# Half-array matmuls of a two-block layer: the later half issued first, the other half queued directly behind it

## The chip, the cores and the metric

The kernel runs on one core of a Trainium2 chip. The metric is the device time of one execution in microseconds (us). The core's engines are PE (TensorE, the matmul array; PEld is its weight load), DVE (VectorE), ACT (ScalarE), POOL (GpSimd) and SP (SyncE). Each engine works through its own queue of instructions in order, and semaphores order one engine against another.

## The reference

256 tokens of width 1024, float32, go through two blocks. What matters here:

```python
# first block: x += 0.5*ffn1(x); mixer = attention + mLSTM; x += 0.5*ffn2(x); norm
scores = einsum('bnqhgd,bnkhd->bhgnqk', qb, kb) * 64**-0.5   # window 128, 16 heads, 4 kv heads, width 64
probs  = softmax(concat([scores, sink]))[..., :-1]
out    = einsum('bhgnqk,bnkhd->bnqhgd', probs, vb)
sc     = einsum('bhtd,bhsd->bhts', q_, k_) * w_intra         # mLSTM, 8 heads, q/k width 64, values 128
...
# second block: mixer = gated linear attention + latent attention; cross attention; ffn with conv
sc = einsum('bhqd,bhkd->bhqk', qi, kf) * 96**-0.5            # latent attention, 8 heads
p  = softmax(where(causal, sc, -inf))
o  = einsum('bhqk,bhkd->bqhd', p, vf)                        # values of width 64
```

## The kernel before

The kernel is one long chain of matmuls. Every dense weight is read from memory as float32 (SP's queue, tiles `wr`), split into a high part `wh` on ACT (line 376) and a low part `wl` on DVE (line 377), and multiplied in two or three matmuls (lines 396 to 407). The tiles `wr`, `wh` and `wl` rotate over six buffers each. Between these weight matmuls stand the small matmuls of the attentions and of the mLSTM.

Four places use only half of the 128 by 128 array, because a head has width 64. They come in pairs, one half for each of two heads:

- Line 719, the first attention's scores. The contraction has 64 rows, rows 0 to 63 for h = 0 and 64 to 127 for h = 1. The two heads write two PSUM banks, `ps[0]` and `ps[1]`.
- Line 759, the first attention's values. The contraction has all 128 rows, and the output has 64 columns of the array, partitions 0 to 63 of `po` for h = 0 and 64 to 127 for h = 1. The moving operand `pTs[2 * kb + h]` is 512 wide. It is written by ACT (line 753), which copies four transposes (line 751) out of PSUM; the copy for h = 1 comes after that for h = 0.
- Line 868, the mLSTM's products of queries and keys, again 64 rows for each head.
- Line 1245, the latent attention's values, 64 columns for each head, with three matmuls of 128 columns per head; the moving operand `pTs[i]` is copied by ACT (line 1240) after the transposes of line 1238.

Lines 1298 and 1322 are half- or quarter-array matmuls of the gated linear attention that the change leaves as they are.

These matmuls are float32 and each stands as two records in the trace: the 12 value matmuls of line 759 are 24 records, the 32 score matmuls of line 719 are 64. The weight matmuls are one record each.

What sets the order of the work: the program is written in the order of the code, and the framework (`TileContext(..., schedule_with_timeline_sim=True)`) then puts each engine's instructions into a fixed order by simulating when each one could run. It may put instructions of other stages between two that stand next to each other in the code. `tc.issue_after(ins)` adds an edge for this placing: what is written inside the block comes later than `ins` in the queue of the same engine. It adds no semaphore. PSUM is two tiles `mm` of two banks each for the weight matmuls and four banks `at` for the small ones.

The first attention runs in four units (p, b), two kv heads each; `scores` of the next unit is written ahead of `values` of the current one. Its matmuls stand between the weight matmuls of the mLSTM's projections. The latent attention does the same with four pairs of heads.

Of the kernel before, what the change touches and what calls it, by code (L numbers as in the profile page):

```python
# [19 lines left out]
P = 128  # L20
D = 1024
KD = D // P
T = 256
# [164 lines left out]
class Builder:  # L188
# [135 lines left out]
                                fill=0.0, base=0, channel_multiplier=-1)  # L324

    @contextmanager
    def queued(self, *engines):

        done = self.nc.cur_bb.bb.instructions
        with ExitStack() as st:  # L330
            for e in engines:
                st.enter_context(self.tc.issue_after(next(i for i in reversed(done) if i.engine == e.engine)))
            yield
# [178 lines left out]
    def mean(self, acc, tag):  # L512

        ps = self.pa()
        self.sums(ps, 0, acc)
        v = self.tmp([P, TB], tag, bufs=1)
        self.nc.vector.tensor_scalar(v, ps[:, :TB], 1.0 / D, None, ALU.mult)
        return v

    def sums(self, ps, i, acc):  # L520

# [138 lines left out]
    def mix(self):  # L660
        nc = self.nc
# [3 lines left out]
        with self.phase("mix") as mp:  # L665
# [20 lines left out]
            aq = [[], []]  # L686
# [4 lines left out]
            ak = biased(product("ak", "ak"), 8)  # L691
            av = mt([P, TB, 256], "av")
            zg = mt([P, TB, 16], "zg")
            bb = self.row("b_av", 0, 272, "bb")
            ps = self.lin_n("av", 272, xs)
# [12 lines left out]
            def scores(p, b):  # L708
                nk = P * (b + 1)
                Ss = mt([P, 2, 4, T], ("ya", "nu")[b])  # L710
                Ss = [Ss[:, h] for h in range(2)]
                ms = [self.tmp([P, 4], "m4", bufs=4) for h in range(2)]
                per = 512 // nk
                for g in range(4 // per):
                    ps = [self.pa() for h in range(2)]
                    for i in range(per):
                        for h in range(2):
                            hs = slice(64 * h, 64 * h + 64)
                            nc.tensor.matmul(ps[h][:, i * nk:i * nk + nk], aq[p][g * per + i][hs, b * P:b * P + P],  # L719
                                             ak[p][hs, 0:nk], start=True, stop=True)  # L720
                    for h in range(2):
                        for i in range(per):
                            j = g * per + i
                            nc.vector.tensor_tensor_reduce(
                                Ss[h][:, j, :nk], ps[h][:, i * nk:i * nk + nk], wm[:, P * (1 - b):2 * P], 0.125, -3.0e38,
                                ALU.add, ALU.max, ms[h][:, j:j + 1])
                for h in range(2):
                    S, m, kv = Ss[h], ms[h], 2 * p + h
                    nm = self.tmp([P, 4], "nm4")
                    nc.vector.scalar_tensor_tensor(nm, m, -1.0, nsink[:, 4 * kv:4 * kv + 4], ALU.mult, ALU.min)  # L730
                    es = self.tmp([P, 4], "es4")
                    nc.vector.tensor_tensor(es, nm, sink[:, 4 * kv:4 * kv + 4], ALU.add)
                    nc.scalar.activation(es, es, AF.Exp)
                    l = self.tmp([P, 4], "l4")
                    for j in range(4):
                        nc.scalar.activation(S[:, j, :nk], S[:, j, :nk], AF.Exp, bias=nm[:, j:j + 1],
                                             accum_out=l[:, j:j + 1])
                    nc.vector.tensor_tensor(l, l, es, ALU.add)
                    r = self.tmp([P, 4], "r4")
                    nc.vector.reciprocal(r, l)  # L740
                    for j in range(4):
                        nc.vector.tensor_scalar(S[:, j, :nk], S[:, j, :nk], r[:, j:j + 1], None, ALU.mult)
                return Ss

            def values(p, b, Ss):
                pTs = []
                for kb in range(b + 1):
                    for h in range(2):
                        pt = self.pa()
                        for j in range(4):  # L750
                            nc.tensor.transpose(pt[:, j * P:j * P + P], Ss[h][:, j, kb * P:kb * P + P], self.ident)  # L751
                        pT = self.tmp([P, 512], "pT", bufs=4)
                        nc.scalar.activation(pT, pt, AF.Copy)
                        pTs.append(pT)
                po = self.pa()
                for kb in range(b + 1):
                    for h in range(2):
                        kv = 2 * p + h
                        nc.tensor.matmul(po[64 * h:64 * h + 64, :], av[:, kb, kv * 64:kv * 64 + 64], pTs[2 * kb + h],  # L759
                                         start=kb == 0, stop=kb == b)  # L760
                self.split(ao[:, :, 4 * p:4 * p + 4, b * P:b * P + P], po.rearrange("p (j t) -> p j t", j=4))

            units = [(p, b) for p in range(2) for b in range(TB)]
# [13 lines left out]
            ps = self.pa()  # L777
# [7 lines left out]
            ps = self.pa()  # L785
# [12 lines left out]
            ps = self.pa()  # L798
# [53 lines left out]
            def weights(m):  # L852

                qt, kt_ = qk[m], qk[4 + m]
                Ws = []
                for h in (2 * m, 2 * m + 1):
                    pw = self.pa()
                    nc.tensor.matmul(pw[:, :3 * P], self.nident[:, h:h + 1].to_broadcast([40, P]), MH, start=True, stop=False)
                    nc.tensor.matmul(pw[:, :3 * P], self.identb, self.kmask.rearrange("p a k -> p (a k)"), start=False, stop=True)
                    W = self.tmp([P, 3 * P], "W", bufs=4)  # L860
                    nc.scalar.activation(W[:, 0:T], pw[:, 0:T], AF.Exp, bias=ga[:, 0, h:h + 1])
                    nc.scalar.activation(W[:, T:3 * P], pw[:, T:3 * P], AF.Exp, bias=ga[:, 1, h:h + 1])
                    Ws.append(W)
                pq = [self.pa() for r in range(2)]
                for a, b, c in ((0, 0, 0), (T, P, P)):
                    for r in range(2):
                        hs = slice(64 * r, 64 * r + 64)
                        nc.tensor.matmul(pq[r][:, a:a + T - b], kt_[hs, b:b + P], qt[hs, c:T], start=True, stop=True)
                for r in range(2):
                    nc.vector.tensor_tensor(Ws[r], pq[r][:, :3 * P], Ws[r], ALU.mult)  # L870
                return Ws
# [195 lines left out]
    def mix2_heads(self, mp, ot, xs, ms):  # L1067
# [165 lines left out]
        def values(hp, Ss):  # L1233
# [7 lines left out]
                pTs.append(pT)  # L1241
            po = self.pa()
            for q0, kb, first, last in ((0, 0, True, True), (P, 0, True, False), (P, 1, False, True)):
                for i in range(2):
                    nc.tensor.matmul(po[64 * i:64 * i + 64, q0:q0 + P], vv[:, kb, 2 * hp + i, :],
                                     pTs[i][:, kb * P + q0:kb * P + q0 + P], start=first, stop=last)
            ms[4 + hp] = ot([P, 2, T], f"mla{hp}", dt=F32R)
            self.split(ms[4 + hp], po[:, :T])

# [64 lines left out]
        st = [None]  # L1314
# [283 lines left out]
```

## Time and profile before

| | |
|---|---|
| median of 3 runs | 1010.16 us (1008.42 to 1011.41) |
| profiled execution | 1012.14 us, of which the trace's span is 1010.4 us |
| PE busy | 992.1 us, 98% of the span |
| DVE / ACT busy | 735.5 us (73%) / 595.2 us (59%) |
| granted TensorE clock, mean | 0.996 |

The trace's times are microseconds from the start of the span. Busy time of PE is the union of its records. A record begins when its matmul starts and lasts until its result is out, so records overlap, and how long a stretch of matmuls takes is read from the start of one row to the start of the next.

### The profile page before, as it was taken

Reading aid. Unit: us, or ns where it says so; the run is one execution under the profiler, and the core shown is the slowest. Engines: PE = TensorE matmul, PEld = TensorE weight load, DVE = VectorE, ACT = ScalarE, POOL = GpSimd, SP = SyncE. Lnnn points to the kernel's source line nnn. Section 1 sums busy time; section 2 is a strip of 40 time slices with the busy share of each in tenths; the row PEclk is TensorE's granted clock in tenths of the full one; section 3 lists DMA queues with packets and bytes.
Section 4 is the critical chain, followed back from the end, with each engine's and each line's share of the span. In section 5 each row is a group of like instructions: output and inputs, shape, how many; then the busy total and the mean of one; then the engine's idle time right before and its main releaser. Section 6 shows DMA issues by size and latency. Waiting matters only on the chain.

```text
span 1010.4 us, 15824 instructions
## 1 busy us (share of the span) xinstructions
PE 992.1 (98%) x5884; PEld 857.2 (85%) x5884; DVE 735.5 (73%) x1289; ACT 595.2 (59%) x1038; POOL 58.3 (6%) x195
## 2 busy tenths in 40 slices
PE   8999999999999999999999999999899999999998
PEld 6888888988677788888888888998688888888887
DVE  6787766668986577776777756768868676998662
ACT  7665544568854556545655644659746465766531
POOL 2100000010000010001000100012001201000000
PEclk9999999999999999999999999999999999999999
DMA  8755555555345335545565655556206235555550
GB/s 307 247 194 187 175 180 178 198 165 181 122 154 188 104 130 204 187 168 174 180 206 189 219 172 185 170 192 211 82 19 211 105 129 204 187 188 178 178 166 21
DMA packets 51405, 172.80 MB, mean 171 GB/s; under 512 B 6256, under 2 KB 7552, under 8 KB 51328
## 3 DMA queue, kind: packets, MB, share of 16 engines
q1 hardware_dynamic: 49536, 169.89, 49.7%
q10 hardware_dynamic: 1728, 1.88, 0.7%
q8 instruction: 46, 0.75, 0.3%
q14 instruction: 31, 0.25, 0.1%
q0 software_dynamic: 64, 0.02, 0.0%
HBM read 170.72 MB, written 1.05 MB: 170 GB/s over the span
## 4 chain that ended last, share of the span: by engine, by line
PE 95%; DVE 2%; ACT 1%; DMA 1%; issue 0%; DVEq 0%; SPq 0%; ACTq 0%
PE mm L400 42%; PE mm L401 21%; PE mm L405 3%; PE mm L406 3%; PE mm L407 3%; PE mm L397 3%; PE mm L396 3%; PE mm L398 3%; PE at L400 1%; PE at L759 1%; PE at L719 1%; DVE wl L377 1%; DMA wr<-in_wts 1%; PE at L401 1%; ACT wh L376 1%; PE at L751 1%
## 5 line engine op out<-in xcount | busy, mean ns | idle before, releaser
L377 DVE TENSOR_TENSOR wl<-wr,wh 128x1024 fp32r<-128x1024 f32 (+5 forms) x376 | 389.6, 1047 | 200.5 <-ACT wh L376 199.1
L376 ACT ACTIVATE wh<-wr 128x1024 fp32r<-128x1024 f32 (+5 forms) x376 | 339.0, 918 | 320.6 <-PE mm L400 159.1
L400 PE MATMUL mm<-xs,wh 128*128 128x512 f32 x1264 | 446.9, 397 | 0.0
L401 PE MATMUL mm<-xs,wl 128*128 128x256 f32 x1264 | 355.2, 281 | 0.8 <-DVE wl L377 0.8
L400 PEld LDWEIGHTS mm<-xs,wh 128*128 128x128 f32 x1264 | 237.6, 188 | 56.8 <-issue 0.7
L401 PEld LDWEIGHTS mm<-xs,wl 128*128 128x128 f32 x1264 | 239.0, 189 | 1.6 <-DVE wl L377 1.1
L400 PE MATMUL mm<-ahl,wh 128*128 128x512 f32 x396 | 140.1, 399 | 0.0
L401 PE MATMUL mm<-ahl,wl 128*128 128x256 f32 x396 | 111.2, 281 | 0.0
L400 PEld LDWEIGHTS mm<-ahl,wh 128*128 128x128 f32 x396 | 74.4, 188 | 18.6
L401 PEld LDWEIGHTS mm<-ahl,wl 128*128 128x128 f32 x396 | 74.8, 189 | 0.0
L406 PE MATMUL mm<-wl,xs 128*128 128x512 f32 (+2 forms) x160 | 61.0, 381 | 0.0
L405 PE MATMUL mm<-wh,xs 128*128 128x512 f32 (+2 forms) x160 | 61.0, 381 | 0.0
L407 PE MATMUL mm<-wh,xs 128*128 128x512 f32 (+2 forms) x160 | 60.7, 379 | 0.0
L400 PE MATMUL mm<-b,wh 128*128 128x512 f32 x128 | 45.4, 395 | 0.0
L397 PE MATMUL mm<-ahl,wh 128*128 128x256 f32 x132 | 37.4, 283 | 0.0
L396 PE MATMUL mm<-ahl,wh 128*128 128x256 f32 x132 | 37.4, 283 | 0.0
L398 PE MATMUL mm<-ahl,wl 128*128 128x256 f32 x132 | 37.3, 283 | 0.0
L401 PE MATMUL mm<-b,wl 128*128 128x256 f32 x128 | 36.5, 285 | 0.0
L406 PEld LDWEIGHTS mm<-wl,xs 128*128 128x128 f32 x160 | 30.1, 188 | 6.2 <-issue 1.1
L405 PEld LDWEIGHTS mm<-wh,xs 128*128 128x128 f32 x160 | 30.1, 188 | 6.1 <-issue 1.1
L407 PEld LDWEIGHTS mm<-wh,xs 128*128 128x128 f32 x160 | 30.1, 188 | 5.8 <-issue 0.8
L400 PEld LDWEIGHTS mm<-b,wh 128*128 128x128 f32 x128 | 24.0, 188 | 5.3
(540 smaller groups left out, 1444.2 us busy)
## 6 DMA issues: line engine op xcount, KB each, us to landing
wr<-in_wts SPq DMA_DIRECT2D x288, 512.0 KB, 4.2
wr<-in_wts SPq DMA_DIRECT2D x26, 384.0 KB, 3.3
wr<-in_memt SPq DMA_DIRECT2D x4, 512.0 KB, 4.2
wr<-in_wts SPq DMA_DIRECT2D x4, 432.0 KB, 3.2
bb<-in_rows ACTq DMA_DIRECT2D x6, 256.0 KB, 4.6
wr<-in_wts SPq DMA_DIRECT2D x4, 272.0 KB, 2.6
x<-in_xt SPq DMA_DIRECT2D x4, 256.0 KB, 4.8
first<-in_wts SPq DMA_DIRECT2D x4, 256.0 KB, 5.0
```

Of the source, the lines that this page charges most:

```text
L376: nc.scalar.activation(hi[:, i:i + m], v[:, i:i + m], AF.Copy)
L377: nc.vector.tensor_tensor(lo[:, i:i + m], v[:, i:i + m], hi[:, i:i + m].bitcast(F32), ALU.subtract)
L396: mm(ps, wh, xs[:, 0, :], start=start, stop=False)
L397: mm(ps, wh, xs[:, 1, :], start=False, stop=False)
L398: mm(ps, wl, xs[:, 0, :], start=False, stop=stop)
L400: mm(ps, wh, xs, start=start, stop=False)
L401: mm(ps[:, T:], wl, xs[:, 0, :], start=False, stop=stop)
L405: mm(ps, xh, wh, start=start, stop=False)
L406: mm(ps, xh, wl, start=False, stop=False)
L407: mm(ps, xl, wh, start=False, stop=stop)
L719: nc.tensor.matmul(ps[h][:, i * nk:i * nk + nk], aq[p][g * per + i][hs, b * P:b * P + P], ak[p][hs, 0:nk], start=True, stop=True)
L751: nc.tensor.transpose(pt[:, j * P:j * P + P], Ss[h][:, j, kb * P:kb * P + P], self.ident)
```

## The change

At the four places the two matmuls of a pair are now written by a helper, `both`, that writes the matmul of half 1 first and then that of half 0 inside `issue_after` of the first. Operands, shapes and results are the same, and so is the number of instructions on every engine. The scheduler then places the rest of the program anew around the pairs.

```diff
+    def behind(self, ins):
+
+        with ExitStack() as st:
+            for i in ins:
+                st.enter_context(self.tc.issue_after(i.ins))
+            yield
...
+    def both(self, mm):
+
+
+        first = mm(1)
+        with self.behind([first]):
+            mm(0)
...
                     for i in range(per):
-                        for h in range(2):
-                            hs = slice(64 * h, 64 * h + 64)
-                            nc.tensor.matmul(ps[h][:, i * nk:i * nk + nk], aq[p][g * per + i][hs, b * P:b * P + P],
-                                             ak[p][hs, 0:nk], start=True, stop=True)
+                        hs = lambda h: slice(64 * h, 64 * h + 64)
+                        self.both(lambda h: nc.tensor.matmul(
+                            ps[h][:, i * nk:i * nk + nk], aq[p][g * per + i][hs(h), b * P:b * P + P], ak[p][hs(h), 0:nk],
+                            start=True, stop=True))
...
                 for kb in range(b + 1):
-                    for h in range(2):
-                        kv = 2 * p + h
-                        nc.tensor.matmul(po[64 * h:64 * h + 64, :], av[:, kb, kv * 64:kv * 64 + 64], pTs[2 * kb + h],
-                                         start=kb == 0, stop=kb == b)
+                    kv = lambda h: 128 * p + 64 * h
+                    self.both(lambda h: nc.tensor.matmul(po[64 * h:64 * h + 64, :], av[:, kb, kv(h):kv(h) + 64],
+                                                         pTs[2 * kb + h], start=kb == 0, stop=kb == b))
...
                 for a, b, c in ((0, 0, 0), (T, P, P)):
-                    for r in range(2):
-                        hs = slice(64 * r, 64 * r + 64)
-                        nc.tensor.matmul(pq[r][:, a:a + T - b], kt_[hs, b:b + P], qt[hs, c:T], start=True, stop=True)
+                    hs = lambda r: slice(64 * r, 64 * r + 64)
+                    self.both(lambda r: nc.tensor.matmul(pq[r][:, a:a + T - b], kt_[hs(r), b:b + P], qt[hs(r), c:T],
+                                                         start=True, stop=True))
...
             for q0, kb, first, last in ((0, 0, True, True), (P, 0, True, False), (P, 1, False, True)):
-                for i in range(2):
-                    nc.tensor.matmul(po[64 * i:64 * i + 64, q0:q0 + P], vv[:, kb, 2 * hp + i, :],
-                                     pTs[i][:, kb * P + q0:kb * P + q0 + P], start=first, stop=last)
+                self.both(lambda i: nc.tensor.matmul(po[64 * i:64 * i + 64, q0:q0 + P], vv[:, kb, 2 * hp + i, :],
+                                                     pTs[i][:, kb * P + q0:kb * P + q0 + P], start=first, stop=last))
```

PE's queue before, at the end of the second unit of the first attention: twelve transposes (only the last four stand here), the four value matmuls of `at_2571`, scores of the fourth unit, the first weight matmul after them. `pT_2548` and `pT_2562` belong to h = 0, `pT_2555` and `pT_2569` to h = 1; `at_2581` and `at_2591` are banks of h = 0, `at_2582` of h = 1.

```order
L751 MATMUL at_2564<-ident,nu_2412 128x128 x4
L759 MATMUL at_2571<-pT_2548,av_2271 64x512
L759 MATMUL at_2571<-pT_2555,av_2271 64x512
L719 MATMUL at_2581<-ak_2265,aq_335_2152 128x256 x2
L759 MATMUL at_2571<-pT_2562,av_2271 64x512
L719 MATMUL at_2582<-ak_2265,aq_335_2152 128x256 x2
L759 MATMUL at_2571<-pT_2569,av_2271 64x512
L719 MATMUL at_2591<-ak_2265,aq_345_2214 128x256 x2
L405 MATMUL mm_2997<-wh_3000,xs_232_1513 128x512
```

The same place in PE's queue with the change (line 751 is now 766, 759 is 773, 719 is 733, 405 is 413):

```order
L766 MATMUL at_2564<-ident,nu_2412 128x128 x4
L773 MATMUL at_2571<-pT_2555,av_2271 64x512
L773 MATMUL at_2571<-pT_2548,av_2271 64x512
L733 MATMUL at_2582<-ak_2265,aq_335_2152 128x256 x2
L733 MATMUL at_2581<-ak_2265,aq_335_2152 128x256 x2
L773 MATMUL at_2571<-pT_2569,av_2271 64x512
L773 MATMUL at_2571<-pT_2562,av_2271 64x512
L733 MATMUL at_2592<-ak_2265,aq_345_2214 128x256 x2
L413 MATMUL mm_2997<-wh_3000,xs_232_1513 128x512
```

The halves of both value pairs and of one pair of scores now stand next to each other, where before a matmul of the other kind stood between them. The scores of `at_2592` still stand without their other half, `at_2591`, which comes 23 weight matmuls later.

PE's queue before, in the latent attention at the first pair of heads: transposes of the probabilities (`S`), products of the gated linear attention (line 1298), the first value matmul of `at_7176` (h = 0), scores of the fourth pair of heads. The five other value matmuls of `at_7176` follow four rows below this piece.

```order
L1238 MATMUL at_7164<-ident,S_1201_6863 128x128 x3
L1298 MATMUL mm_7296<-qz_7003,g2k_7007 64x64 x8
L1238 MATMUL at_7170<-ident,S_1205_6877 128x128
L1245 MATMUL at_7176<-pT_1269_7168,vv_6704 64x128
L1216 MATMUL at_7326<-kT_7050,qT_7043 128x128
L1217 MATMUL at_7326<-kT_7050,qT_7043 128x256
L1216 MATMUL at_7340<-kT_7050,qT_7043 128x128
L1217 MATMUL at_7340<-kT_7050,qT_7043 128x256
L1238 MATMUL at_7170<-ident,S_1205_6877 128x128 x2
L1298 MATMUL mm_7303<-qz_7003,g2k_7007 64x64 x8
```

The same place with the change (1238 is now 1252, 1298 is 1311, 1245 is 1258):

```order
L1252 MATMUL at_7164<-ident,S_1201_6863 128x128 x3
L1252 MATMUL at_7170<-ident,S_1205_6877 128x128 x3
L1311 MATMUL mm_7296<-qz_7003,g2k_7007 64x64 x8
L1311 MATMUL mm_7303<-qz_7003,g2k_7007 64x64 x8
L1258 MATMUL at_7176<-pT_1271_7174,vv_6704 64x128
L1258 MATMUL at_7176<-pT_1269_7168,vv_6704 64x128
```

The six value matmuls of a pair of heads now stand in one run, half 1 and half 0 by turns (the first two stand here), and so in all four pairs of heads; before, the first one stood alone in three of the four. The transposes and products around them moved together as well. In the whole program PE changes between whole-array and half-array work 47 times, against 62 before. SP's and POOL's queues are the same as before; DVE's and ACT's change order within the two attentions.

## Rows read from the trace of the kernel before

**Rows 1.** the page, engines: busy us (share of the span) xinstructions

```profile
PE 992.1 (98%) x5884; PEld 857.2 (85%) x5884; DVE 735.5 (73%) x1289; ACT 595.2 (59%) x1038; POOL 58.3 (6%) x195
```

**Rows 2.** windows: stretch, its us, busy us (xrecords) by engine, clock, DMA

```profile
255.00:265.00 10.00, 10.00 (x63) 6.65 (x61) 10.00 (x33) 7.44 (x14) 0.00 (x0) 1.00 0.46 158
...
719.00:731.00 12.00, 11.03 (x106) 8.89 (x105) 11.10 (x42) 9.61 (x29) 0.00 (x0) 1.00 0.01 2
```

**Rows 3.** timeline of PE, first unit: start us, us to last end, what, xrecords

```profile
255.66 1.07 PE L759 MATMUL at<-pT,av 128*64 128x512 f32 x2
256.67 0.94 PE L719 MATMUL at<-ak,aq 64*128 64x128 f32 x12
257.53 1.07 PE L759 MATMUL at<-pT,av 128*64 128x512 f32 x2
...
258.96 0.66 PE L751 MATMUL at<-ident,nu 128*128 128x128 f32 x4
```

**Rows 4.** timeline of PE, end of the second unit

```profile
263.98 1.35 PE L759 MATMUL at<-pT,av 128*64 128x512 f32 x4
265.26 1.13 PE L719 MATMUL at<-ak,aq 64*128 64x256 f32 x4
266.32 1.07 PE L759 MATMUL at<-pT,av 128*64 128x512 f32 x2
...
270.44 0.50 PE L405 MATMUL mm<-wh,xs 128*128 128x512 f32 x1
```

**Rows 5.** timeline of ACT, copies of the second unit

```profile
263.63 0.58 ACT L753 ACTIVATE pT<-at 128x512 f32<-128x512 f32 x1
```

**Rows 6.** timeline of PE, end of the third unit

```profile
291.02 1.07 PE L759 MATMUL at<-pT,av 128*64 128x512 f32 x2
292.02 0.49 PE L407 MATMUL mm<-wh,xs 128*128 128x512 f32 x1
292.45 1.07 PE L759 MATMUL at<-pT,av 128*64 128x512 f32 x2
293.45 0.50 PE L405 MATMUL mm<-wh,xs 128*128 128x512 f32 x1
293.79 0.40 PE L406 MATMUL mm<-wl,xs 128*128 128x512 f32 x1
294.02 0.39 PE L407 MATMUL mm<-wh,xs 128*128 128x512 f32 x1
```

**Rows 7.** timeline of PE, fourth unit, first value matmul

```profile
304.55 1.07 PE L759 MATMUL at<-pT,av 128*64 128x512 f32 x2
305.55 0.50 PE L406 MATMUL mm<-wl,xs 128*128 128x512 f32 x1
```

**Rows 8.** timeline of PE, fourth unit, the other three value matmuls

```profile
309.63 1.93 PE L759 MATMUL at<-pT,av 128*64 128x512 f32 x6
311.49 0.39 PE L778 MATMUL at<-sp,tri 128*128 128x8 f32 x2
```

**Rows 9.** timeline of PE, mLSTM, one half alone (line 868)

```profile
327.84 0.92 PE L868 MATMUL at<-qk,qk 64*128 64x256 f32 x4
328.68 0.39 PE L401 MATMUL mm<-b,wl 128*128 128x256 f32 x1
```

**Rows 10.** timeline of PE, mLSTM, both halves in one run

```profile
335.15 0.93 PE L868 MATMUL at<-qk,qk 64*128 64x256 f32 x8
336.01 0.50 PE L400 MATMUL mm<-b,wh 128*128 128x512 f32 x1
```

**Rows 11.** timeline of PE, latent attention, first pair of heads

```profile
721.08 0.43 PE L1245 MATMUL at<-pT,vv 128*64 128x128 f32 x2
721.44 0.49 PE L1216 MATMUL at<-kT,qT 96*128 96x128 f32 x2
...
724.65 0.87 PE L1245 MATMUL at<-pT,vv 128*64 128x128 f32 x10
725.45 0.64 PE L1201 MATMUL at<-ident,q 128*96 128x128 f32 x4
```

More of the change, by code (lines that the diff above doesn't have):

```diff
@@ L326, in queued @@
     @contextmanager
+    def behind(self, ins):
[3 more added lines that the diff above has]
+            yield
+    @contextmanager
     def queued(self, *engines):
```

## The prediction, made before the changed kernel ran

> **What bounds the kernel now.** I read the engines' busy shares first. PE is busy 98% of the span [rows 1], so a microsecond less of PE's own work is a microsecond less of time, unless another engine then holds PE up. Next I read the busy time by stretch at the two places where the change acts. In the first attention (255 to 265 us) PE is busy all of the time, at a granted clock of 1.00, but so is DVE; in the latent attention (719 to 731) PE idles 1.0 us and DVE only 0.9 of 12 [rows 2]. So PE sets the pace, with DVE close behind it in the attentions. Last I read PE's timeline around the half-array matmuls, where starts of following rows give what a run costs.
>
> **What a run of half-array matmuls costs.** A value matmul of the first attention (two records) alone takes 1.00 us: 255.66 to 256.67 [rows 3], and again 291.02 to 292.02 [rows 6] and 304.55 to 305.55 [rows 7]. Three of them in one run, halves 1, 0, 1, take 1.86 us [rows 8], not 3 x 1.00. Two records have a start of 0.43 of their own each (1.86 less 1.00, for the two records of one matmul), so the six records filled four places: the first two matmuls ran beside each other. The same in the products of the mLSTM: one half alone, four records, takes 0.84 us; both halves, eight records, take 0.86 [rows 9, 10]. So the other half is free if it stands next to its partner with its input there, and costs a full run if something of another shape stands between.
>
> Changing shape costs too. The one weight matmul between the two value runs of the third unit takes 0.43 us from start to start, and that after the second run 0.34, where the next takes 0.23 [rows 6]. So one half-array run more puts about 0.1 to 0.2 us on the whole-array work around it.
>
> For the value pairs a rule of the Trainium skill speaks against this. "TensorE: Matmul & The Clock Gate", Part 3, under "The mechanism", says that a weight load overlaps running matmuls only when the row group differs, and the two value halves use the same rows. By that rule the value pairs would stay serial and the sum would be that of rival B. The trace disagrees: six records in 1.86 us [rows 8].
>
> **The change part by part.** The number of instructions stays the same on every engine; what goes is time in which half of the array stands empty.
>
> First unit. Before: 255.66 to 258.96 = 3.30 us for value half 0, twelve score records, value half 1, four score records [rows 3]. After: the value pair 1.00, then sixteen score records in one run. Twelve take 0.86 and the four after the second value 0.43 (257.53 to 258.96 less 1.00); in one run the four are two places of 0.11 more, so 1.09. New 2.09, saved 1.21.
>
> Second unit. Before: 263.98 to 270.44 = 6.46 us [rows 4] for two value matmuls, scores half 0 (1.06), value (1.00), scores half 1, value, scores of half 0 of the next bank pair. After: pair 1.00, both halves of the scores 1.06, pair 1.00, one half of scores 1.06 = 4.12. Saved 2.34. But half 1 now comes first, and its copy ends at 263.63 + 0.58 = 264.21 [rows 5], 0.23 after PE got there; in the run of 1.28 us that opens [rows 4] half 0 hid this. I take 0.2 off: 2.1. The wait could be nothing (ACT now copies the two in a row) or both copies in full, 1.16.
>
> Third unit. Before: 291.02 to 294.02 = 3.00 us for two value matmuls and three weight matmuls [rows 6]. After: 1.00 + 0.34 + 0.23 + 0.23 = 1.80. Saved 1.2.
>
> Fourth unit. Before: 1.00 + 1.86 [rows 7, 8] and a change of shape of 0.1. After: two pairs of 1.00 and one small matmul between them that was behind them, so 0.2 for its changes of shape. Saved 0.8.
>
> Scores of the first two units (lines 719) and the mLSTM's products: the same runs as before with halves 0 and 1 exchanged. Where a run held both halves they ran together with half 0 first [rows 10]; with half 1 first I take the same. Where the two halves stood apart, they still do. Nothing, with bounds of 0.8 us either way per run (the price of a half alone [rows 9]).
>
> Latent attention. Before, three of the four pairs of heads have one value matmul alone, 0.36 us [rows 11], and two changes of shape around it, 0.2. The other five take 0.80 in one run of ten records [rows 11]; with the sixth there are three full pairs in the same six places, again 0.80. Saved 3 x 0.56 = 1.7. Here DVE has 0.9 us to spare in twelve [rows 2], and the softmax rows it makes are what PE transposes next. I take 0.4 back: 1.3. Bounds: 1.9, and 0 if DVE sets the pace throughout.
>
> What is queued behind the new waits. A pair waits at the head of PE's queue for the copy of its half 1, and everything on PE stands behind it: the scores, whose readers are DVE's masked maxima, and the weight matmuls, whose readers free the buffers of ACT and DVE. In the new order of the first, third and fourth unit 21 or more weight matmuls stand between the transposes and the pair, nearly 5 us at 0.23 each [rows 6], against two copies of 0.58 [rows 5]; only the second unit and the latent attention are tight. SP's and POOL's queues stay as they were, so no transfer is moved.
>
> The sum: 1.2 + 2.1 + 1.2 + 0.8 + 1.3 = 6.6 us. Against the profiled execution, 1012.14 (span 1010.4 and 1.7 around it), that is 1005.5. That execution lies 2.0 above the median of the runs, 1010.16; from the median it is **1003.6 us**, 0.65% less. A difference under 0.3%, 3 us, can't be told from no change here (the three runs before lie within 3.0 us).
>
> **The rivals.**
>
> A, another engine takes the gain back. DVE has no idle time from 255 to 265 [rows 2]. If PE gets ahead by 5 us and then waits for the softmax of the next unit, what stays is the saving at the places where DVE has room. For it: the full DVE. Against it: PE shows no idle time there before, and the scheduler has moved DVE's rescaling of the probabilities forward. If all of the second unit's 2.1 and the latent attention's 1.3 go, and half of the first's, 2.6 is left: 1007.6, about the edge of no change. 0.14.
>
> B, the value halves do not run beside each other after all, and the run of rows 8 is a quirk. Then only the joined scores gain (1.06 in the second unit) and some ten changes of shape at 0.1: 1010.16 - 2.1 = 1008.1. Against it: two different shapes agree [rows 8, 10]. 0.04. The rule of the Trainium skill told above ("TensorE: Matmul & The Clock Gate", Part 3) would give this time.
>
> C, slower: the wait at the head of the queue. There are ten value pairs or runs with such a wait (six in the first attention, four in the latent one). If PE reaches each before either copy has begun, it stands for two copies, 1.16 us [rows 5], or 11.6 in all; with the 6.8 that the pairs give, 1010.16 + 4.8 = 1015.0. It is slower by over 0.3% from a mean wait of 0.98 us on. For it: in the second unit the copy ends 0.23 late already. Against it: ACT works in the meantime on nothing that PE needs earlier, and the other units have many weight matmuls in front. 0.08.
>
> D, the change doesn't do what it says: `issue_after` sets the order, but lets other work in between. It still does at two pairs of scores. At the value pairs both halves stand together in the queue, so this is left with the small chance of a PE that loses the pairing when half 1 leads by two matmuls: no scores gain, 1004.7, within the forecast.
>
> **How the numbers follow.** Forecast 0.74, within 1001.5 to 1006.8 (all of the 6.6 kept and 2 us more, or half of it kept). A 0.14, B 0.04, C 0.08. The range over these that leaves out C and the far ends of the others is 1000.8 to 1008.4. Faster by over 0.3% (under 1007.1): 0.72 of the forecast and 0.04 of A, 0.76. Slower: C, less where it only cancels the gain, 0.07. No change: the rest, 0.17.
>
> **What would show it.** Line 773 (759 before) with its 24 records in six runs of four at two records' time, about 6 us instead of 10 in sum; one x8 row of scores in the second unit at 1.06 us; line 1258 in four rows of x12 of 0.8 us. PE idle in the windows 245 to 315 and 719 to 745 no more than before, about 1.5 us in the second. Wrong: value rows of x4 that last 1.9 us (B), or idle times in front of lines 773, 1258, 766 or 1252 that sum to several us (C, A).

## The result and the profile after

The changed kernel takes 1003.6 us (median of six runs, 1001.02 to 1007.92) against 1011.05 for the kernel before (six runs beside them, 1008.42 to 1011.73). The ratio is 0.9943, with a 95% interval of 0.9923 to 0.9964: 5.8 us less, 3.6 to 7.8. (The two medians lie 7.4 apart; the ratio is the estimate that is used here.) The forecast was 1003.6, in a range of 1000.8 to 1008.4. That forecast and median agree to a tenth is chance: the forecast took 6.6 us from 1010.16, and the ratio gives 5.8 from 1011.05. How the time got there differs from the sum in two terms, as the rows show.

The profiled execution took 1001.02 us (span 999.3), 11.1 less than that of before. PE is still busy 98% of the time, for 12.6 us less than in [rows 1]:

```profile
PE 979.5 (98%) x5884; PEld 851.8 (85%) x5884; DVE 735.5 (74%) x1289; ACT 595.2 (60%) x1038; POOL 59.5 (6%) x195
```

The first two units of the first attention, on PE's timeline (start, us to the last end, line and tiles, records; idle time before in brackets), where [rows 3, 4] stood before:

```profile
255.61 1.08 PE L773 MATMUL at<-pT,av 128*64 128x512 f32 x4
256.62 1.16 PE L733 MATMUL at<-ak,aq 64*128 64x128 f32 x16
257.71 0.66 PE L766 MATMUL at<-ident,nu 128*128 128x128 f32 x4
...
260.39 1.31 PE L766 MATMUL at<-ident,nu 128*128 128x128 f32 x8 [0.42 <-DVE b L503]
261.63 1.08 PE L773 MATMUL at<-pT,av 128*64 128x512 f32 x4
262.64 1.14 PE L733 MATMUL at<-ak,aq 64*128 64x256 f32 x8
263.71 1.08 PE L773 MATMUL at<-pT,av 128*64 128x512 f32 x4
264.72 1.13 PE L733 MATMUL at<-ak,aq 64*128 64x256 f32 x4
266.28 0.50 PE L413 MATMUL mm<-wh,xs 128*128 128x512 f32 x1 [0.43 <-DVE zc L569]
```

A pair of value matmuls (x4) now takes 1.01 us, 255.61 to 256.62, as long as one alone did; the sixteen score records take 1.09. What is new are idle times in front of other work. They stand in the windows too (stretch, its us, busy us by engine as PE, PEld, DVE, ACT, POOL, granted clock, DMA): PE now loses 0.4 us in each stretch where DVE is full, the first of which it filled in [rows 2]:

```profile
255.00:265.00 10.00, 9.58 (x64) 5.59 (x63) 10.00 (x33) 6.38 (x11) 0.00 (x0) 1.00 0.48 158
265.00:275.00 10.00, 9.57 (x41) 7.14 (x41) 10.00 (x42) 9.89 (x33) 0.00 (x0) 1.00 0.23 69
```

A third wait, 0.55 us, stands at 250.95, for an earlier L569. DVE's own timeline says why PE waits: the operations that free the banks (a subtraction in line 503, an addition in line 569) come in DVE's queue behind other work, and end at 250.89, 260.33 and 266.23.

```profile
249.06 1.23 DVE L385 TENSOR_TENSOR wl<-wr,wh 128x1024 fp32r<-128x1024 f32 x1 [2.32 <-ACT wh L384]
250.21 0.68 DVE L569 TENSOR_TENSOR zc<-mm,zc 128x512 f32<-128x512 f32 x1
...
258.46 1.28 DVE L836 SCALAR_TENSOR_TENSOR qk<-zc,cols,qk 128x256 f32<-128x256 f32 x3
259.64 0.69 DVE L503 TENSOR_TENSOR b<-at,b 128x512 fp32r<-128x512 f32 x1
...
265.54 0.69 DVE L569 TENSOR_TENSOR zc<-mm,zc 128x512 f32<-128x512 f32 x1
```

So TensorE idles 1.41 us in the first attention, where it never did before. The wait at 250.95 lies 4.7 us ahead of the first value pair, where nothing had been gained yet, and behind a DVE that had itself just waited 2.32 us for ACT: it comes from the new order of the queues and not from a full DVE.

The third and fourth unit on PE's timeline, for [rows 6 to 8]:

```profile
285.24 1.08 PE L773 MATMUL at<-pT,av 128*64 128x512 f32 x4
286.25 0.50 PE L414 MATMUL mm<-wl,xs 128*128 128x512 f32 x1
286.59 0.39 PE L415 MATMUL mm<-wh,xs 128*128 128x512 f32 x1
...
303.93 1.08 PE L773 MATMUL at<-pT,av 128*64 128x512 f32 x4
304.94 0.39 PE L792 MATMUL at<-sp,tri 128*128 128x8 f32 x2
305.25 1.08 PE L773 MATMUL at<-pT,av 128*64 128x512 f32 x4
```

The latent attention on PE's timeline, for [rows 11]: the first run of twelve takes 0.80 us (714.62 to 715.42), as forecast; two of the others last as long, and the fourth takes 0.88 to the next row. But the waits around them grew, from 1.4 us in four (0.40, 0.38, 0.15 and 0.47) to 2.1 in five, of which three are shown:

```profile
714.62 0.88 PE L1258 MATMUL at<-pT,vv 128*64 128x128 f32 x12
715.42 0.49 PE L1230 MATMUL at<-kT,qT 96*128 96x128 f32 x2
...
721.66 0.67 PE L1366 MATMUL mm<-st,qz 128*128 128x256 f32 x2 [0.80 <-issue]
...
730.80 0.88 PE L1258 MATMUL at<-pT,vv 128*64 128x128 f32 x12 [0.26 <-ACT pT L1254]
...
734.48 0.39 PE L404 MATMUL mm<-mla,wh 128*128 128x256 f32 x1 [0.48 <-ACT mla L502]
```

**Where the 11.1 us are.** Both kernels issue the same 5240 weight matmuls, so the starts of the same one in both traces cut the span into stretches that can be compared. The last column is a second execution of the changed kernel's order of instructions (experiment no_queueing, below).

| stretch (us in the kernel before) | before | after | second execution |
|---|---|---|---|
| 0 to 230, first feed-forward | 230.0 | -2.9 | -1.4 |
| 230.0 to 318.0, first attention | 87.93 | -3.64 | -3.63 |
| 318 to 440, with the mLSTM | 122.2 | +0.1 | +0.1 |
| 440 to 650, second feed-forward | 210.0 | -1.2 | -1.2 |
| 650.16 to 746.29, latent attention | 96.14 | 0.0 | -0.1 |
| 746 to 817 | 70.4 | +0.3 | +0.3 |
| 816.7 to 821.3, start of the third feed-forward | 4.7 | -1.5 | -1.6 |
| 821 to the end | 189.0 | -2.2 | +0.1 |

Only three of these rows hold places of the change: the first attention, the mLSTM and the latent attention. Most of the rest comes from two habits of TensorE that the runs brought out; the 0.3 us from 746 to 817 is not explained.

The first is its granted clock, read by windows. Of before, and then of after:

```profile
714.50:718.50 4.00, 4.00 (x19) 3.44 (x19) 2.63 (x14) 1.99 (x9) 2.32 (x11) 0.57 0.37 126
817.00:820.50 3.50, 3.50 (x12) 2.97 (x11) 3.50 (x11) 3.31 (x8) 0.00 (x0) 0.51 0.72 219
```

```profile
706.00:712.50 6.50, 5.88 (x23) 5.34 (x24) 4.87 (x19) 4.05 (x15) 2.32 (x11) 0.51 0.24 81
809.50:813.00 3.50, 3.50 (x21) 3.04 (x21) 3.50 (x13) 3.43 (x8) 0.00 (x0) 1.00 0.74 240
```

Both places follow an idle time of PE that both kernels have (3.24 us in the latent attention, 2.26 in front of the third feed-forward). Before, the clock fell to its lower level, 1.2 GHz, for 3.4 us at each; after, for 6.8 us at the first and not at all at the second, where 21 records now fit into 3.5 us instead of 12. That is the -1.5 of the table. What the clock cost in the latent attention, where PE also waits for other engines, is read below from latent_undone and values_only.

The second is the rate of the dense stretches, told at the end.

### The profile page after: what moved, and what is told of

It is laid out like the page before. It is cut to its first block, busy times and chain, and to the rows that moved or that the text cites. A ratio compares the mean times of both kernels' runs of the same rounds, so it can differ in the third digit from the quotient of the medians.

```text
span 999.3 us, 15822 instructions
## 1 busy us (share of the span) xinstructions
PE 979.5 (98%) x5884; PEld 851.8 (85%) x5884; DVE 735.5 (74%) x1289; ACT 595.2 (60%) x1038; POOL 59.5 (6%) x195
## 4 chain that ended last, share of the span: by engine, by line
PE 89%; DVE 6%; ACT 2%; issue 1%; DMA 1%; POOL 0%; DVEq 0%; SPq 0%; ACTq 0%
PE mm L408 41%; PE mm L409 21%; PE mm L414 3%; PE mm L413 3%; PE mm L415 3%; PE mm L405 3%; PE mm L404 3%; PE mm L406 3%; DVE wl L385 3%; PE at L408 1%; ACT wh L384 1%; DMA wr<-in_wts 1%; PE at L409 1%; DMA cols<-in_cols 0%; PE at L881 0%
## 5 line engine op out<-in xcount | busy, mean ns | idle before, releaser
L408 PE MATMUL mm<-ahl,wh 128*128 128x512 f32 x396 | 137.4, 394 | 0.0
```

What stands on the lines that cost most here:

```text
L408: mm(ps, wh, xs, start=start, stop=False)
```

## The experiments

Ratios are to the kernel before on the same chip, with 95% intervals; five rounds each. "Its first attention" and "its latent attention" are the stretches of the table, 87.93 and 96.14 us before, 84.29 and 96.13 after.

**Which half of the edit does it: no_queueing, half0_first.**

```
 def both(self, mm):                    # no_queueing
-    first = mm(1)
-    with self.behind([first]):
-        mm(0)
+    mm(1)
+    mm(0)
...
-    first = mm(1)                      # half0_first
+    first = mm(0)
     with self.behind([first]):
-        mm(0)
+        mm(1)
```

> All four places later half first as in the changed kernel, but the other half is not queued directly behind. The order of instructions on all five engines comes out the same as that of the changed kernel, so this is also a second execution of it. Theory (the order of the halves alone makes the pairs): 1003.6 us, ratio 0.994. Rival (the queueing does it): ratio 1.000. For the stretch from 15 to 180 us, in which TensorE runs the same matmuls in all these kernels without a wait, the theory that the rate of matmuls differs by execution says that its length varies by up to 2% among these four runs, with no relation to the edit; the rival that the changed kernel makes it shorter says that only this run has the changed kernel's 2.4 us less.

> The changed kernel with half 0 first at all four places and half 1 queued directly behind it. The order of instructions on all five engines comes out the same as that of the kernel before, so it is also a third execution of that. Theory (which half goes first makes the pairs, the queueing adds nothing): ratio 1.000, the first attention's stretch 87.9 us as before and not 84.3. Rival (queueing one half behind the other is enough): ratio 0.995, 84.3 us. For the stretch from 41 to 186 us, where both executions of the kernel before ran at 176.7 ns and both of the changed kernel's order at 173.3: 176.7 again if the kernel sets the rate, either one if the execution does.

no_queueing: 1004.8 us, ratio 0.9956 (0.9943 to 0.9969), first attention 84.30. half0_first: 1010.33 us, 1.0007 (0.9991 to 1.0023), first attention 87.97. The queueing does nothing here: without it the order on all five engines is that of the changed kernel, and with half 0 first and half 1 queued behind it is that of the kernel before. A matmul can only be queued behind one that is there; half 0, whose copy is made first, goes as soon as it can, and other work slips in before half 1. When half 1 leads, half 0 is ready too.

**Is it the half of the array or the order of readiness: mirrored.**

```
-                    for h in range(2):
+                    for h in (1, 0):
                         pt = self.pa()
...
-                    self.both(lambda h: nc.tensor.matmul(...
+                    self.both0(lambda h: nc.tensor.matmul(...     # mm(0), then mm(1)
```

(the same at the latent attention's values)

> As the changed kernel, but at both kinds of values the transposes and copies of half 1 are made first, and the matmul of half 0 goes first: the half whose input is made last still leads, though it is now the earlier half of the array. Theory (what makes the pair is that the half whose input comes last leads, so that both are ready): the same runs, four records of half-array values in 1.0 us and twelve of the latent attention in 0.80, and the time of the changed kernel, 1003.6 to 1004.8, ratio 0.995. Rival (the later half of the array has to be loaded first for the two to run together): four records in 1.86 us, twelve in 1.46, and the time of the kernel with neither kind paired, about 1009, ratio 1.000.

1003.76 us, 0.9942 (0.9920 to 0.9964), first attention 84.34, latent 96.37. On PE's timeline a pair takes 1.00 us and a run of twelve 0.81, with half 0 of the array leading:

```profile
262.64 1.08 PE L779 MATMUL at<-pT,av 128*64 128x512 f32 x4
263.64 1.14 PE L739 MATMUL at<-ak,aq 64*128 64x256 f32 x8
...
723.82 0.88 PE L1264 MATMUL at<-pT,vv 128*64 128x128 f32 x12
724.63 0.49 PE L1236 MATMUL at<-kT,qT 96*128 96x128 f32 x2
```

What matters is that the half whose input is made last leads, whichever half it is.

**Must the halves alternate: apart_in_run.**

```
-                for kb in range(b + 1):
-                    self.both(lambda h: nc.tensor.matmul(po[64 * h:64 * h + 64, :], ...
+                for h in (1, 0):
+                    for kb in range(b + 1):        # each queued behind the last
+                        last = [nc.tensor.matmul(po[64 * h:64 * h + 64, :], ...
```

> As the changed kernel, but within one bank of values all matmuls of half 1 go before all of half 0: 1, 1, 1, 0, 0, 0 in the latent attention and 1, 1, 0, 0 where the first attention has two pairs. The runs stay as long in records. Theory (two matmuls share a place only where they are neighbours of different halves): the twelve records of the latent attention fill five places of 0.22 instead of three, 1.24 us instead of 0.80; in the second and fourth unit one value matmul stands alone (1.00 us) and three follow as halves 1, 0, 0 in 1.86 instead of two pairs of 1.00 each. The first attention is 1.7 us longer than in the changed kernel, the latent one 0 to 1.8 (its waits may hide it): 1005.3 to 1008, ratio 0.998. Rival (the array takes the halves in any order, as long as they stand in one run): 0.80 and 1.4, no change of time.

1004.81 us, 0.9946 (0.9929 to 0.9963); too near to the changed kernel for the runs to part them, but the stretch does. First attention 85.61, 1.32 longer, with one of the three DVE waits (0.43) gone: 1.7 of PE's time, as expected. Its PE timeline:

```profile
266.59 1.94 PE L776 MATMUL at<-pT,av 128*64 128x512 f32 x6
268.46 0.91 PE L733 MATMUL at<-ak,aq 64*128 64x256 f32 x3
...
729.82 1.14 PE L1264 MATMUL at<-pT,vv 128*64 128x128 f32 x12
730.90 0.49 PE L1233 MATMUL at<-kT,qT 96*128 96x128 f32 x2
```

Halves 1, 0, 0 take 1.87 us. 1, 1, 1, 0, 0, 0 take 1.08, in all four runs, where the alternating run takes 0.80; 1.24 had been expected. The latent stretch is 96.67. So the value halves lose when they do not alternate, but 1.08 is nearer to four places (1.02) than to the five that the theory gives, so more than the one pair of neighbours shared a place.

For the scores the theory that only neighbours share a place is out. The second unit's scores stand in the changed kernel's queue as halves 1, 1, 0, 0 (`at_2582` twice, `at_2581` twice, in the section on the change), and their x8 row takes 1.07 us (262.64 to 263.71), as long as one half alone [rows 4]. These halves split the rows of the array, those of the values its columns; no run here shows why the two differ.

**One place at a time: values_only, latent_only, scores_mlstm_only.** Each is the changed kernel with the other places as before, such as

```
-                    kv = lambda h: 128 * p + 64 * h
-                    self.both(lambda h: nc.tensor.matmul(po[64 * h:...
+                    for h in range(2):
+                        kv = 2 * p + h
+                        nc.tensor.matmul(po[64 * h:...
```

> Only the value halves of the first attention stand later half first; scores, mLSTM products and latent values are as before. Theory (a half-array matmul is free beside its partner when both are ready, and costs a place of its own otherwise): in the order that results the six value pairs stand together as in the changed kernel, so the value matmuls fill 6 places of 0.86 us instead of 10 (3.4 us) and have three runs fewer (0.4), the scores lose one place of 0.46 and two runs (0.7); but the mLSTM's products, whose halves are not asked to pair, stand in 8 runs instead of 5, 4 places of 0.35 and three fixed parts of 0.14 more (1.8 us lost). Net 2.8 us less than before: ratio 0.997, about 1008.3 us, of which the first attention alone (245 to 310 us) is 4 us shorter. Rival 1 (what joined the value halves is not the pairing; the gain is elsewhere): no shorter stretch there, ratio 1.000. Rival 2 (the mLSTM's halves cost nothing when apart): ratio 0.995, as the whole change but for the latent attention.

> Only the latent attention's value halves stand later half first; up to there the order of the instructions is that of the kernel before. Theory: four runs of twelve records of 0.80 us instead of three of 0.36, three and one of 0.80: 12 places of 0.22 instead of 15 and three runs and changes of shape fewer, 1.1 to 1.5 us less: ratio 0.9986, about 1009.6. Rival (DVE or ACT sets the pace there and takes it back): ratio 1.000, with PE idle between 714 and 745 longer by the same 1.1 to 1.5 us. The stretch up to 700 us should read as in the kernel before whatever the theory.

> Only the scores of the first attention and the mLSTM's products stand later half first; both kinds of values are as before. Theory: these are ready together anyway, so exchanging the halves moves little by itself: by the places in the resulting order (scores 21 instead of 22, values 9 instead of 10, mLSTM products 13 in six runs instead of 12 in five, latent values 16 in eight runs instead of 15 in seven) 0.9 us less, ratio 0.999, about 1010. Rival (the scores carry the gain of the second unit, as the queueing of the other half behind was meant for them): 2 us or more, ratio 0.998 or less.

values_only: 1005.74 us, 0.9961 (0.9943 to 0.9980). The first attention takes 83.93, 4.0 less: the value pairs are enough for all that the whole change gains there. From 318 to 440 us 3.0 are lost again: the mLSTM's products stand in eight runs, each of one half alone like [rows 9], instead of five. Three more runs at 0.84 are 2.5, and the rest is changes of shape; 1.8 had been expected. Turning the mLSTM's halves round too would not mend that: in the order of instructions that results they stay in eight runs (not run). With the scores turned round as well, as in the changed kernel, there are five, as before.

latent_only: 1009.92 us, 1.0002 (0.9986 to 1.0018): no gain where 1.1 to 1.5 had been expected. The rival named waits, and PE's idle time did grow by 1.3 us. Not foreseen was the clock, which stood at 0.50 for two times 3.4 us: PE's own work fell by only 0.5, and the latent stretch took 96.94.

scores_mlstm_only: 1007.98 us, 0.9993 (0.9978 to 1.0008), in line with the 0.9 us expected, though the rival of 2 us lies at the edge of the interval. The stretches decide: its first attention took 86.80, 1.1 less, the rest up to 440 us 0.5 more, and the latent stretch 97.04, 0.9 more. The 4.0 of values_only and this 1.1 do not add up: together they give 3.64.

**Did DVE take the gain of the first attention back: act_rescale.**

```
                     for j in range(4):
+                        if h and b:
+                            nc.scalar.activation(S[:, j, :nk], S[:, j, :nk], AF.Copy, scale=r[:, j:j + 1])
+                        else:
-                        nc.vector.tensor_scalar(S[:, j, :nk], ...
+                            nc.vector.tensor_scalar(S[:, j, :nk], ...
```

> As the changed kernel, but in the units with two blocks of keys ACT does the rescaling of half 1's four probability rows (0.28 us each on DVE) in place of DVE, 1.1 us of DVE's work in each of two units. Theory (the first attention gives 3.4 to 3.5 us and not 5.3 because DVE, full there, is late three times, 0.55 + 0.42 + 0.43 us of TensorE's idle time): two or three of these waits go, up to 1.4 us less than the changed kernel, 1002.5 us. Rival (the waits come from the order in which DVE and ACT take their work, so that a lighter DVE moves them to ACT): the idle time of TensorE between 245 and 285 us stays at 1.4 us or more, no gain.

1002.65 us, 0.9934 (0.9914 to 0.9955), not to be told from the changed kernel; first attention 83.74, 0.55 less. One wait went (266.28). The first stayed (0.54), and the second turned into a longer one, for ACT, on PE's timeline:

```profile
253.72 0.50 PE L408 MATMUL mm<-xs,wh 128*128 128x512 f32 x1 [0.54 <-DVE zc L569]
...
262.93 1.50 PE L769 MATMUL at<-ident,nu 128*128 128x128 f32 x12 [0.69 <-ACT pT L771]
```

Idle time fell from 1.41 to 1.24 us, which is 0.17 of the 0.55; the rest is PE's own work in another order. Mostly the rival, then: what PE waits for is the place of the freeing instruction in a queue, more than DVE's load. From 318 to 440 us 1.3 are lost, as the mLSTM's products came out in six runs instead of five.

**What the latent attention gave: latent_undone, filled_paired, filled_unpaired.** latent_undone puts back the two loops of the latent attention alone. The filled kernels add to the changed kernel, and to latent_undone, six matmuls that nobody reads:

```
         q1 = turned(1)
+        fill = self.pa()
+        for _ in range(6):          # each queued behind the last on TensorE
+            nc.tensor.matmul(fill, self.ident, self.wmask.rearrange("p a k -> p (a k)"), start=True, stop=True)
```

> The changed kernel with the latent attention's value halves back as before; up to there the order of the instructions on every engine is that of the changed kernel. The stretch read is the one between two weight matmuls, the one that starts at 642.52 us in the changed kernel and the one that starts at 738.65: 96.13 us there, 96.07 in its second execution (the kernel without the queueing), 96.14 in the kernel before. Theory 1 (the latent attention's pace is set by the chain of ACT and DVE and by where TensorE waits for it, and pairing gives nothing there): 95.2 us, as in the kernel with the first attention's values alone, whose order there is the same; the whole is 0 to 1 us faster than the changed kernel, about 1003 us, ratio 0.995. Theory 2 (the pairing gives its 1.3 us there and something else took them): 97.4 us, the whole 1.3 us slower than the changed kernel.

> The changed kernel with six matmuls of 128x512 whose result nobody reads (0.43 us each at full clock, 2.6 us) put into TensorE's idle 3.24 us ahead of the second pair of scores of the latent attention. Stretch as for latent_undone (96.13 us in the changed kernel, 96.14 in the kernel before). Theory (the pairing gave its 1.3 us in the latent attention, but the granted clock read 0.50 for 6.8 us there instead of the 3.4 us of the kernel before, which took 1.5 us back; TensorE's idle time opens these episodes): no reading of 0.50 in the stretch, 93.0 to 94.0 us long, the whole about 2.5 us less than the changed kernel, 1001 to 1002, ratio 0.992. Rival (the clock costs nothing there, since ACT and DVE set the pace): the clock stays up, the stretch stays at 95.5 to 96.1. Second rival (the episodes come from something else): readings of 0.50 remain.

> The same six idle matmuls in the kernel with the latent attention's halves back as before. Its stretch was 95.01 us without them, where its profile showed no reading under 1.00. Theory (with the clock up, pairing is worth 1.3 us there): 94.5 to 95.2 us, 1.0 to 1.8 longer than the filled paired kernel. Rival (pairing is worth nothing there, the chain through ACT and DVE decides): within 0.3 us of the filled paired kernel.

latent_undone: 1002.17 us, 0.9926 (0.9908 to 0.9943), the fastest of the kernels run, though its interval still overlaps that of the changed kernel. Its latent stretch took 95.01, as theory 1 said. Its window after the same idle 3.24 us, and then the same stretch of work in values_only:

```profile
706.00:712.50 6.50, 4.73 (x41) 3.85 (x43) 5.59 (x23) 4.80 (x17) 2.47 (x11) 1.00 0.25 81
```

```profile
711.72:718.22 6.50, 5.78 (x39) 5.03 (x40) 5.23 (x21) 4.79 (x17) 2.34 (x11) 0.74 0.27 81
```

In latent_undone the clock stayed up: 41 records in 6.5 us where the changed kernel had 23, but PE then waited 1.1 us for DVE and ACT in it. values_only has the same order of instructions in the latent stretch on PE, DVE and ACT, and its clock stood at 0.50 for 3.4 us; its stretch took 95.15. So in this order the clock's 3.4 us were worth 0.14: PE's own work took 1.4 us less with the clock up, and its idle time 1.2 more. At the start of the third feed-forward, where PE is busy all of the time (817.00 to 820.50), the same 3.4 us cost 1.5.

One more thing can be read here. The kernel before has the same seven runs of value halves as values_only and the same 3.4 us at 0.50, and takes 96.14. The order of the small matmuls around the runs is thus worth 1.0 us by itself, as much as was expected of the pairing.

filled_paired: 1006.0 us, 0.9955 (0.9940 to 0.9969). The clock never fell in the latent stretch, in either filled kernel, which fits the theory that the idle time opens these episodes (latent_undone shows that not every such idle time does). But I had mis-sized the fill: each of the six is two records of 0.44.

```profile
705.60 5.42 PE L1270 MATMUL at<-wmask,ident 128*128 128x512 f32 x12 [0.61 <-DVE m L1236]
710.86 0.39 PE L1230 MATMUL at<-kT,qT 96*128 96x128 f32 x2
```

It filled 5.3 us where 2.6 were meant, and the stretch came to 95.58. filled_unpaired: 1005.29, 0.9951 (0.9933 to 0.9968), 98.14, with the same fill and the clock up as well. So with fill and clock alike the paired order is 2.6 us shorter; 1.0 to 1.8 had been expected, and both stretches came out longer than expected. 0.5 of that is idle time of PE (2.42 against 2.93 in the stretch); the rest is PE's own work, and agrees with four runs more in the unpaired order, eight against four, at 0.36 each [rows 11] and a change of shape. The rival (nothing) is out for these two kernels. They are not the changed kernel, though: the fill is 2 us longer than the idle time it was to fill, and PE idles 2.4 us in the stretch instead of 5.4, so more of PE's own work turns into time. A fill of the right length was not run.

**The comparison with itself: before_again.** No edit.

> The kernel before, unchanged, once more: ratio 1.000 within the interval. Theory (the weight matmuls of the long dense stretches run at 173.3 or 176.7 ns each, by execution and not by kernel): its stretches from 41 to 186, 562 to 633 and 850 to 996 us are at either rate, not all three at 176.7 as in the profile of before, and its span lies 1 to 7 us under that profile's 1010.4. Rival (the order of the kernel before sets the slow rate): all three at 176.7 again. The latent attention's readings of 0.50 last 0, 3.4 or 6.8 us, by execution too.

1009.55 us, 0.9998 (0.9985 to 1.0012). First attention 87.93, latent 96.16 with 3.4 us at 0.50, as in the profile shown. Of the three dense stretches one (562 to 633) was at the other rate and two at the same; the span lay only 0.7 below.

## Why the prediction was right, and where it was not

**The pairs.** Right, to a hundredth: first unit 2.10 us (2.09 forecast), second 4.22 without its wait (4.12), third 1.81 (1.80), fourth two pairs of 1.01. Line 773 stands in six rows of x4, line 1258 in four of x12. The wait of 0.23 for half 1's copy, for which 0.2 was taken off, did not come: no row of 773 has an idle time before it.

**Scores and mLSTM at nothing.** Right for this kernel, but not a property of the edit: in values_only the mLSTM's regrouping cost 3.0 us.

**First attention 5.3 in sum; it gave 3.64.** PE's own work fell by 5.05 us (87.93 to 82.88); 1.41 came back as waits. The step that failed is rival A's "Against it": that PE showed no idle time there before, and that DVE's rescaling had been moved forward. PE now waits for DVE three times. Rival A had this in kind, but it looked for waits for the next unit's softmax, and the waits are for banks that are freed late; one of them comes from the new order alone. Rival A also priced the loss at 4.0 us over both attentions, all or nothing, when a part of it belonged into the sum.

**Latent attention 1.3; it gave 0.0.** The runs of line 1258 are what was forecast. The step that failed is "I take 0.4 back": the forecast let most of PE's saved work turn into time, and its own lower bound, 0 if another engine sets the pace, was the nearer case. PE's waits grew by 0.7, and the clock, which the sum left out, stood at 0.50 for 6.8 us there instead of 3.4. How much of the gain each of the two took stays open: in the unpaired order 3.4 us of low clock were worth 0.14, and no two executions of the paired order differ in their clock. What the runs do show is that the unpaired order of latent_undone and values_only takes 95.0 to 95.2, 1.0 less than the changed kernel, and that pairing gives 2.6 where the fill leaves PE less idle time.

**The total.** The places of the change gave 3.5 and 3.6 us in the two profiled executions. 1.5 came in both from the clock that stayed up at the start of the third feed-forward, which no step spoke of, and 0.3 went from 746 to 817. Together 4.8 us, inside the interval of 3.6 to 7.8; the other 6.3 of the 11.1 between the two profiles lie in the dense stretches, whose rate changes from one execution to the next. The forecast's 6.6 lies inside it as well, so the runs alone would not have told that two terms were off by 3 us, or that a stroke of luck covered half of it.

**Rivals.** B: a pair in 1.01 us excludes it. The rule of the Trainium skill ("TensorE: Matmul & The Clock Gate", Part 3), by which a weight load overlaps running matmuls only when the row group differs, does not hold here: these column halves use the same rows, and a pair takes as long as one half alone. That the value matmuls would run one after the other was the prediction's own conclusion from that rule. C: PE waits once before a run of twelve, 0.26 us, and never before a first-attention pair; 11.6 was its price. D: the queueing does nothing, as no_queueing shows, yet the pairs stand.

## What to carry to other kernels

Let the half whose input is made last lead, and a scheduler that issues whatever is ready will set both halves side by side; queueing the second behind the first added nothing in these runs. Count a gain on a full engine net of what the next engine frees late: here 1.4 of 5.3 us. Where a stretch begins with an idle TensorE, compare the granted clock before comparing the kernels, and ask whether PE waits there anyway: the same 3.4 us at the lower level cost 1.5 us in one stretch and 0.14 in another.

## What had not been expected of the hardware

In the dense feed-forward stretches PE is busy all the time at a granted clock of 1.00, and yet its weight matmuls run at one of two rates. The window from 60 to 180 us of before, before_again, half0_first (three executions of one order), after and no_queueing (two of the other), all with the same sequence of matmuls:

```profile
60.00:180.00 120.00, 120.00 (x681) 104.03 (x680) 83.21 (x121) 63.29 (x80) 0.00 (x0) 1.00 0.54 183
```

```profile
60.00:180.00 120.00, 120.00 (x683) 104.19 (x682) 82.98 (x120) 63.16 (x81) 0.00 (x0) 1.00 0.58 183
```

```profile
60.00:180.00 120.00, 120.00 (x702) 105.29 (x701) 84.69 (x123) 64.11 (x82) 0.00 (x0) 1.00 0.60 190
```

```profile
60.00:180.00 120.00, 120.00 (x702) 105.29 (x701) 84.69 (x123) 64.12 (x82) 0.00 (x0) 1.00 0.56 189
```

```profile
60.00:180.00 120.00, 120.00 (x697) 105.07 (x697) 84.36 (x123) 64.42 (x82) 0.00 (x0) 1.00 0.59 189
```

The (x...) behind PE's busy time is the count of records. The windows cut slightly different pieces out of the sequence, so the starts are the better measure: on average 176.7 ns from one to the next in the first two and 173.3 in the other three, with the same distance in both halves of the window (176.5 and 176.9 against 173.2 and 173.5). The third is the kernel before's order at the faster rate, so it is the execution that sets it here; nor is it the chip, for values_only (176.7) and no_queueing (173.3) ran on the same one. From 850 to 996 us, counted where a 512-column and a 256-column matmul alternate, the changed kernel's order ran at either rate (173.3 in one execution, 176.7 in the other), and that of before at 176.7 in all three. At 1.9% such stretches of some 360 us (41 to 186, 562 to 633, 850 to 996) can differ by 7 us, more than the change is worth. What sets the rate stays open, and so does whether the order of before is more prone to the slow one.
